# Conditioning blocks of a decoder layer: four visits of eight in place of six of five and six

## The chip, the cores and the metric

The kernel runs on one core of a Trainium2 chip. The metric is the device time of one execution in microseconds; the time before is the median of three runs. One more execution was profiled, and every row below comes from its trace.

## What is computed

One inference step of a one-layer decoder for 256 prompt tokens and 8 x 4 sample tokens (288 columns), model width 2048, all in float32. Cut to what matters here:

```python
mod = (silu(c) @ w_ada + b_ada).reshape(n, 6, 1, 2048)      # c: 9 conditioning vectors
sh_m, sc_m, gt_m, sh_f, sc_f, gt_f = [mod[:, i] for i in range(6)]
h = rms(x, g_mix) * (1 + sc_m) + sh_m
b_gate, c_gate, hc, u, v, ga, gb = split(h @ w_in)
ya = b_gate * conv(c_gate * hc)                              # short causal convolution
yb = gelu(u) * (w_causal @ rms(gelu(v), g_v) + b_sg)         # mixing within chunks
merged = sigmoid(ga) * (ya @ w_pa) + sigmoid(gb) * (yb @ w_pb)
x = x + gt_m * (merged @ w_out)
h2 = rms(x, g_ffn) * (1 + sc_f) + sh_f
gate, up = split(h2 @ w_ffn_in)
x = x + gt_f * ((silu(gate) * up) @ w_ffn_out)               # then a last rms
```

`mod` has 96 tiles of 128 features. Tiles 32 to 47 are gt_m, wanted first by the residual behind w_out, and tiles 48 to 63 are sh_f.

## The kernel before

Features lie on the 128 partitions, tokens along the free dimension. Weights are streamed from HBM once. A main block (`Blk`) is a piece of a weight matrix of up to 16 tiles of 128 x 128, 1 MB. It is loaded into a buffer of the pool `raw` (`RAW = 7` buffers of 8 KB per partition, L28), and then split into a high and a low half in four quarters of four tiles: ScalarE casts the high half (L480), VectorE subtracts to get the low half (L487). For each half there are four buffers of one quarter (`SPB = 4`, L478 and L481), so the next block's quarters take over the buffers that the present block's matmuls give back. Each tile then makes three matmuls of 288 columns (L239, L242, L244), 48 in a block, and a sink on VectorE (L802 for the blocks around the change) takes the finished sum from PSUM.

A conditioning block (`Ada`) is 1 MB of `w_ada` too and takes a `raw` buffer, but it isn't split: four float32 matmuls of 512 columns (L412, eight instructions in the trace) read the raw buffer as it is, into column groups 0 to 3 of one accumulator `ada`. Units a2 (tiles 32 to 47) and a3 (tiles 48 to 63) have 16 blocks each. They are done in *visits*: a run of conditioning blocks between two main blocks. Units a4 and a5 are done in a visit of six and a later one of ten, whose last four blocks are fetched by `fetch` (L392) into other buffers (the pool `kept`).

What sets the order: `steps2` lists the main blocks of this stage (first two half blocks wE and wF, then wD, pa, pb, wo), and `at` puts `plan[n]` behind the n-th of them. PE's order is the order of the steps, by hand. The loads (SyncE, one queue), ScalarE and VectorE are put in order by the framework's planner here, from when a buffer would be free and by place in the program. The loop at the end walks over `stream`, all blocks with a `raw` buffer; at its i-th block it emits the load of `order[i + AHEAD]` (`AHEAD = RAW`), then the split of the next main block if that one has a load, then the block's matmuls. `order` is `stream` with four main blocks moved ahead of earlier conditioning units.

Among the steps of the visits stand three others: `v_stats` (row statistics of v, after the 9th main block), `half_gt` (halves gt_m, after the 15th) and `v_samples` (transposes v of the sample tokens and stores it, after the 28th).

Of the kernel before, what the change touches and what calls it, by code (L numbers as in the profile page):

```python
# [88 lines left out]
def decoder_kernel(tc, d):  # L89
    nc = tc.nc  # L90
    from contextlib import ExitStack

    with ExitStack() as es:
        def pool(name, bufs=1, **kw):
            return es.enter_context(tc.tile_pool(name=name, bufs=bufs, **kw))

        pc = pool("const")
        pw = pool("wstream")
        pslot = pool("slots", MAIN)
        pkept = pool("kept", KEPT)  # L100
        ptmp = pool("tmp", 5)
        pps = pool("psum", 4, space=bass.MemoryType.PSUM)
        with tc.manual_schedule(engines={nc.tensor.engine}):
            _body(tc, nc, d, pc, pw, pslot, pkept, ptmp, pps)


def _body(tc, nc, d, pc, pw, pslot, pkept, ptmp, pps):
# [482 lines left out]
    def ada(name):  # L590
        u = units[name]
        return [Ada(u, b) for b in range(16 // u[2])]
# [58 lines left out]
    def pre_h1(k0, k1):  # L651
        def scaled(k):
            def f():
                made[k] = normed(k, S["rb1"])

            return f

        return Do(lambda: jobs.extend(scaled(k) for k in range(k0, k1)), None)
# [91 lines left out]
    def mk_h1(k0, k1):  # L750
        def f():
            gm_of(k0, k1)
            if S.get("paced") is not None:
                return make_h1(k0, k1)
            modulate(range(k0, k1), lambda k: normed(k, S["rb1"]), gm1, 0, h1)

        return Do(f)
# [381 lines left out]
    plan = {4: [Do(root, None)], 5: aC[:2], 6: aC[2:5] + [pre_h1(2, 5)], 7: aC[5:] + [mk_h1(2, 5)]}  # L1139
# [17 lines left out]
    steps2 += [Blk("pb", i, yb.__getitem__, sink_pb) for i in range(8)]  # L1157
    steps2 += [Blk("wo", i, mg.__getitem__, sink_wo) for i in range(16)]
    a2, a3, a4, a5 = ada("a2"), ada("a3"), ada("a4"), ada("a5")
    visits = [u[o:e] for u in (a2, a3) for o, e in ((0, 5), (5, 10), (10, 16))]  # L1160
    visits[1].insert(0, Do(v_stats, None))
    visits[2].append(Do(half_gt))
    visits[4].insert(0, Do(v_samples, None))
    plan = dict(zip((3, 9, 15, 21, 28, 35), visits))

    def apart(unit, plan, second, early):
        plan[second] = unit[6:]
# [19 lines left out]
    plan = {}  # L1187
# [12 lines left out]
    order = list(stream)  # L1200
    for unit, blk in ((aC[:2], wA[3]), (aC[2:5], wA[4]), (aC[5:], wA[5]), (aE[5:11], wC[0])):
        order.remove(blk)
        order.insert(order.index(unit[0]), blk)
    head = contextlib.ExitStack()
    head.enter_context(tc.manual_schedule(engines={A.engine, V.engine, SY.engine}))
    for s in stream[:2]:
# [21 lines left out]
    for s in steps:  # L1228
# [14 lines left out]
        i = pos[id(s)]  # L1243
# [124 lines left out]
```

## Time and profile before

| what | us |
|---|---|
| median of 3 runs | 1591.73 (1591.66 to 1592.06) |
| profiled execution | 1592.19 |
| its span, first to last instruction | 1590.40 |
| TensorE matmul (PE) busy | 1579.8 |
| VectorE (DVE) busy | 1014.4 |
| ScalarE (ACT) busy | 736.2 |

The mean granted clock of TensorE is 0.998 of full speed. In the rows below times are microseconds from the start of the span. A row of the timeline has its start, its length (for several alike instructions in a row the length of all), the engine, the line, the operation, what it writes and reads, the shapes and the count; in brackets stands the idle time of the engine ahead of it and what ended it. SPq is SyncE, which issues the loads. In the rows of a line of code "DMA to landing" is the time from the issue to the moment when the last byte is there, as minimum, median and maximum.

### The profile page before, as it was taken

What the parts mean: (1) busy time and instruction counts of PE and PEld (TensorE: products, weight loads), DVE (VectorE), ACT (ScalarE), POOL (GpSimd) and SP (SyncE); (2) the same over time, 40 slices, a digit from 0 to 9 for tenths busy, and PEclk for the clock granted to TensorE, in tenths of its full rate; (3) what the DMA queues carried; (4) which work ended last, traced back from release to release, by engine and by line L of the source; (5) the groups of instructions that cost most, each with busy time, mean ns of one, the idle gap of its engine ahead of it and who ended that gap; (6) DMA issues with size and microseconds to landing.
All of it is one profiled execution on the core that took longest, in us unless ns stands there. A gap on an engine that the chain in (4) does not pass through costs nothing.

```text
span 1590.4 us, 31810 instructions
## 1 busy us (share of the span) xinstructions
PE 1579.8 (99%) x12700; PEld 1519.9 (96%) x12700; DVE 1014.4 (64%) x2200; ACT 736.2 (46%) x1366; POOL 21.4 (1%) x65
## 2 busy tenths in 40 slices
PE   9999999999999999999999999999999999999997
PEld 8999899998999989899898999999999999999997
DVE  6777788877755758567844555555555555555565
ACT  6633344643444435356643444444444444444464
POOL 0000000000000000011000000000000000000000
PEclk9999999999999999999999999999999999999999
DMA  9887876777767778784757356453564534645341
GB/s 382 333 331 281 306 261 217 276 290 296 291 231 266 309 290 264 273 295 164 295 182 275 128 181 212 161 176 113 171 230 159 176 120 164 231 159 175 113 165 60
DMA packets 67685, 357.89 MB, mean 225 GB/s; under 512 B 7632, under 2 KB 19536, under 8 KB 37840
## 3 DMA queue, kind: packets, MB, share of 16 engines
q1 hardware_dynamic: 67248, 355.73, 61.6%
q8 instruction: 99, 1.62, 0.4%
q14 instruction: 50, 0.41, 0.1%
q10 hardware_dynamic: 288, 0.13, 0.0%
HBM read 352.74 MB, written 3.09 MB: 224 GB/s over the span
## 4 chain that ended last, share of the span: by engine, by line
PE 98%; DMA 1%; DVE 0%; DVEq 0%; ACT 0%; issue 0%; ACTq 0%
PE pm L239 31%; PE pm L244 31%; PE pm L242 30%; PE ada L412 5%; DMA raw<-in_wK 1%; DMA raw<-in_w 0%; DVE st L1079 0%; DMA t<-in_c 0%; PE px L242 0%; PE px L239 0%; PE px L244 0%; PE px L911 0%; PE px L910 0%; PE px L857 0%; PE px L213 0%; PE px L1051 0%
## 5 line engine op out<-in xcount | busy, mean ns | idle before, releaser
L239 PE MATMUL pm<-s,hi 128*128 128x288 f32 (+1 forms) x3750 | 1094.8, 292 | 0.0
L242 PE MATMUL pm<-s,hi 128*128 128x288 f32 (+1 forms) x3750 | 1090.5, 291 | 0.0
L244 PE MATMUL pm<-s,lo 128*128 128x288 f32 (+1 forms) x3738 | 1088.1, 291 | 0.0
L480 ACT CAST hi<-raw 128x512 fp32r<-128x512 f32 (+1 forms) x963 | 585.5, 610 | 777.9 <-PE pm L242 743.5
L487 DVE TENSOR_TENSOR lo<-raw,hi 128x512 fp32r<-128x512 f32 (+1 forms) x849 | 577.5, 682 | 408.6 <-ACT hi L480 396.1
L239 PEld LDWEIGHTS pm<-s,hi 128*128 128x128 f32 x3750 | 702.1, 187 | 11.7 <-issue 9.9
L242 PEld LDWEIGHTS pm<-s,hi 128*128 128x128 f32 x3750 | 702.2, 187 | 0.0
L244 PEld LDWEIGHTS pm<-s,lo 128*128 128x128 f32 x3738 | 699.9, 187 | 0.0
L258 DVE TENSOR_TENSOR lo<-raw,hi 128x512 fp32r<-128x512 f32 x111 | 74.4, 676 | 19.8 <-ACT hi L480 18.7
L412 PE MATMUL ada<-raw,cs 128*32 128x512 f32 (+2 forms) x1088 | 80.7, 444 | 1.0 <-DMA raw<-in_a 0.6
L412 PEld LDWEIGHTS ada<-raw,cs 128*32 128x32 f32 x1088 | 29.1, 110 | 41.9 <-issue 37.5
L802 DVE TENSOR_TENSOR s<-pm,s 128x288 f32<-128x288 f32 x72 | 32.8, 456 | 16.3 <-PE pm L244 16.1
L311 ACT CAST s<-t 128x288 fp32r<-128x288 f32 (+1 forms) x76 | 32.9, 433 | 15.6 <-DVE t L834 9.4
L313 DVE TENSOR_TENSOR s<-t,s 128x288 fp32r<-128x288 f32 (+1 forms) x76 | 35.0, 460 | 6.0 <-ACT s L311 5.2
L353 DVE SCALAR_TENSOR_TENSOR x<-pm,mod,x 128x256 f32<-128x256 f32 x79 | 37.6, 475 | 0.0
L1000 DVE SCALAR_TENSOR_TENSOR t<-t,pm 128x288 f32<-128x288 f32 x42 | 19.1, 455 | 19.6 <-PE pm L244 19.6
L794 DVE TENSOR_TENSOR s<-pm,s 128x288 f32<-128x288 f32 x48 | 21.8, 454 | 10.8 <-PE pm L244 10.0
L352 DVE TENSOR_TENSOR t<-pm,mod 128x32 f32<-128x32 f32 x79 | 15.1, 192 | 20.1 <-PE pm L244 19.5
L779 DVE SCALAR_TENSOR_TENSOR s<-pm,s 128x256 f32<-128x256 f32 x36 | 17.3, 481 | 8.3 <-PE pm L244 8.3
L785 DVE TENSOR_TENSOR s<-s,rb 128x288 f32<-128x288 f32 x48 | 21.6, 449 | 0.0
L181 ACT ACTIVATE t<-x 128x288 f32<-128x288 f32 x29 | 12.9, 444 | 17.6 <-DVE x L356 17.6
L186 DVE TENSOR_TENSOR acc<-acc,t 128x288 f32<-128x288 f32 x33 | 15.0, 455 | 8.2 <-ACT t L181 8.2
(170 smaller groups left out, 489.0 us busy)
## 6 DMA issues: line engine op xcount, KB each, us to landing
raw<-in_fi SPq DMA_DIRECT2D x84, 1024.0 KB, 4.8
raw<-in_a SPq DMA_DIRECT2D x56, 1024.0 KB, 5.0
raw<-in_f SPq DMA_DIRECT2D x64, 704.0 KB, 4.0
raw<-in_wD SPq DMA_DIRECT2D x34, 1024.0 KB, 6.7
raw<-in_aE SPq DMA_DIRECT2D x16, 1024.0 KB, 7.0
raw<-in_wo SPq DMA_DIRECT2D x16, 1024.0 KB, 6.0
raw<-in_wC SPq DMA_DIRECT2D x19, 768.0 KB, 6.5
raw<-in_pa SPq DMA_DIRECT2D x8, 1024.0 KB, 9.7
```

Source lines behind the costliest of these rows:

```text
L239: PE.matmul(out, wh, ah, start=first, stop=False)
L242: end_ = PE.matmul(out, wh, al, start=False, stop=turn and last)
L244: end_ = PE.matmul(out, wl, ah, start=False, stop=last)
L258: lows.pop(0)[1]()
L311: A.copy(hi, a)
L313: V.tensor_tensor(lo, a, hi.bitcast(F32), ALU.subtract)
L353: V.scalar_tensor_tensor(x[:, m, :TP], ps[:, :TP], mod[:, gt0 + m, 0:1], x[:, m, :TP], ALU.mult, ALU.add)
L412: PE.matmul(acc[32 * j : 32 * j + 32, h * w // n : (h + 1) * w // n], cs[:, kt, :], self.held[2 * j + h] if self.held else self.raw[:, o : ...
L480: A.copy(hi, self.raw[:, s * 128 : e * 128])
L487: sub()
L794: return V.tensor_tensor(part[m], ps[:, :T], part[m], ALU.add)
L802: V.tensor_tensor(a, ps[:, :T], a, ALU.add)
```

## The change

The 16 blocks of a2 and of a3 are done in two visits of eight each, behind main blocks 9 and 15 (a2) and 28 and 35 (a3). The visits behind main blocks 3 and 21 are gone. `v_stats`, `half_gt` and `v_samples` keep their places. In the load order, the main block behind each visit is moved ahead of the visit's first conditioning block.

```diff
     a2, a3, a4, a5 = ada("a2"), ada("a3"), ada("a4"), ada("a5")
-    visits = [u[o:e] for u in (a2, a3) for o, e in ((0, 5), (5, 10), (10, 16))]
-    visits[1].insert(0, Do(v_stats, None))
-    visits[2].append(Do(half_gt))
-    visits[4].insert(0, Do(v_samples, None))
-    plan = dict(zip((3, 9, 15, 21, 28, 35), visits))
+    visits = [u[o:e] for u in (a2, a3) for o, e in ((0, 8), (8, 16))]
+    visits[0].insert(0, Do(v_stats, None))
+    visits[1].append(Do(half_gt))
+    visits[2].insert(0, Do(v_samples, None))
+    plan = dict(zip((9, 15, 28, 35), visits))
...
         order.remove(blk)
         order.insert(order.index(unit[0]), blk)
+    for unit in (a2[:8], a2[8:], a3[:8], a3[8:]):
+        i = order.index(unit[-1]) + 1
+        order.insert(order.index(unit[0]), order.pop(i))
```

## Rows read from the trace of the kernel before

**Rows 1.** The page: busy times; the chain by engine; the casts (busy, mean ns)

```profile
PE 1579.8 (99%) x12700; PEld 1519.9 (96%) x12700; DVE 1014.4 (64%) x2200; ACT 736.2 (46%) x1366; POOL 21.4 (1%) x65
PE 98%; DMA 1%; DVE 0%; DVEq 0%; ACT 0%; issue 0%; ACTq 0%
L480 ACT CAST hi<-raw 128x512 fp32r<-128x512 f32 (+1 forms) x963 | 585.5, 610 | 777.9 <-PE pm L242 743.5
```

**Rows 2.** Waits of PE, whole span, largest on a load: total, times, longest (us)

```profile
PE ada L412 <- DMA raw<-in_a: 0.6, 1, 0.6
```

**Rows 3.** Timeline of PE around the visit of five blocks behind main block 21

```profile
413.30 0.29 PE L244 MATMUL pm<-s,lo 128*128 128x288 f32 x1
413.52 4.50 PE L412 MATMUL ada<-raw,cs 128*32 128x512 f32 x40
417.95 0.40 PE L239 MATMUL pm<-s,hi 128*128 128x288 f32 x1
418.19 0.29 PE L242 MATMUL pm<-s,hi 128*128 128x288 f32 x1
```

**Rows 4.** Timeline of PE around the visit of six blocks behind main block 15

```profile
370.71 5.36 PE L412 MATMUL ada<-raw,cs 128*32 128x512 f32 x48
376.00 0.40 PE L239 MATMUL pm<-s,hi 128*128 128x288 f32 x1
```

**Rows 5.** SP's waits, 440 to 466; then two loads, 452.5 and 458.7, to landing

```profile
SPq L463 <- DVE lo L487: 17.4, 3, 5.8
...
DMA to landing us min/median/max: 4.7/4.8/4.8
```

**Rows 6.** Timeline of DVE and PE at the start of two visits (413.52, 463.96)

```profile
415.10 0.69 DVE L487 TENSOR_TENSOR lo<-raw,hi 128x512 fp32r<-128x512 f32 x1
...
463.96 1.04 PE L412 MATMUL ada<-raw,cs 128*32 128x512 f32 x8
...
464.18 1.10 DVE L487 TENSOR_TENSOR lo<-raw,hi 128x512 fp32r<-128x512 f32 x1
465.20 0.47 DVE L884 SCALAR_TENSOR_TENSOR s<-px,r,s 128x256 f32<-128x256 f32 x1
```

**Rows 7.** First two loads inside three visits, timeline of PE and SP, line L463

```profile
328.74 1.07 PE L412 MATMUL ada<-raw,cs 128*32 128x512 f32 x8
329.87 0.33 SPq L463 DMA_DIRECT2D raw<-in_wD  x1
...
L463 SPq DMA_DIRECT2D raw<-in_wD x2: 328/356/383, 329.9 to 330.3; - x2
DMA to landing us min/median/max: 4.9/5.9/7.0
...
L463 SPq DMA_DIRECT2D raw<-in_wD x2: 328/328/328, 371.8 to 372.7; - x2
DMA to landing us min/median/max: 4.7/6.1/7.5
...
L463 SPq DMA_DIRECT2D raw<-in_wD x2: 327/354/382, 465.3 to 466.2; - x2
DMA to landing us min/median/max: 5.0/6.0/7.1
```

**Rows 8.** DVE in the visit behind block 3 and after it: stretch, length, busy

```profile
286.20:290.60 4.40, 3.35 (x10) 1.00 0.51 158
290.60:328.70 38.10, 33.69 (x74) 1.00 0.74 286
```

**Rows 9.** Timeline of PE in a4's visit of ten blocks

```profile
657.78 5.36 PE L412 MATMUL ada<-raw,cs 128*32 128x512 f32 x48
...
666.52 0.40 PE L239 MATMUL pm<-s,hi 128*128 128x288 f32 x1
```

**Rows 10.** PE at the end: stretch, length, busy, granted clock, DMA share, GB/s

```profile
1582.20:1585.00 2.80, 0.00 (x0) 1.00 0.72 277
1585.00:1586.00 1.00, 0.00 (x0) 0.60 1.02 407
```

## The prediction

> **What bounds the kernel now.** I read the busy times first, then the chain that ended last, then the waits of PE, then the timeline around the visits. TensorE is the kernel: it is busy 1579.8 of 1590.4 us and the chain lies on it for 98% [rows 1]. Over the whole span it waited for a load once, a conditioning matmul, 0.6 us [rows 2], at the start of the kernel; in the stretch that is changed it waits for nothing. So nothing can be gained there by making a wait shorter. Time can only come from work that PE no longer does, and any wait that the change makes for PE is added to the end in full, since no later slack exists to take it back.
>
> **What a visit costs PE.** A visit of five blocks starts at 413.52 and the next main matmul at 417.95 [rows 3], 4.43 us; a visit of six takes 370.71 to 376.00, 5.29 us [rows 4]. The difference, 0.86 us, is one block, and the rest of a visit is fixed: from the last main matmul before (413.30) to the second one after (418.19) pass 4.89 us [rows 3], of which five blocks are 4.30 and two ordinary matmul steps 0.26 (six main blocks lie between 376.00 and 413.52 [rows 3, 4], so a main block is 6.25 us and one of its 48 steps 0.13). That leaves **0.33 us per visit** for going into conditioning matmuls and out again. The change has two visits fewer and the same 32 blocks: -0.66 us. That is its whole gain on PE.
>
> **What the transfers cost.** A block of conditioning is 1 MB that PE uses up in 0.86 us. A lone 1 MB transfer takes 4.7 to 4.8 us from issue to landing [rows 5]. So a visit runs from what already lies in the seven raw buffers, and the question is how many of its eight blocks can lie there.
>
> Count them at the moment the visit starts. Between visits SP issues one load per main block, released by the last low half (L487) of a main block (three of them on L463 in those 26 us) [rows 5]: the raw buffer of a main block comes free only when its split is done, and its last quarter waits for a high/low buffer that the matmuls of the block before give back. In the visit at 463.96 this last quarter begins at 464.18, in the one at 413.52 at 415.10 [rows 6], after the visit's start in both. So when a visit starts, one of the seven buffers still holds the main block that follows. Before, the other six hold five or six conditioning blocks, and all are there. After, the main block is put ahead of the eight in the load order, so six blocks (1 to 6) are in and **blocks 7 and 8 have no buffer**. Their loads can be issued only when the visit itself frees one.
>
> When that is, the trace shows: the first load inside a visit leaves at 329.87, 371.8 and 465.3 for visits that start at 328.74, 370.71 and 463.96 [rows 4, 6, 7]. In the first two that is 1.13 and 1.1 us after the start, when the visit's first block, 0.86 us long, has drained; in the third it is 1.3 us, at the end of the low half [rows 6]. It lands 4.7 to 5.0 us later, and the second load lands 2.4 us (330.3 + 7.0 against 329.9 + 4.9), 3.7 us (372.7 + 7.5 against 371.8 + 4.7) and 3.0 us (466.2 + 7.1 against 465.3 + 5.0) after the first [rows 7]. I take 1.13 + 4.8 for block 7 and 3.0 more for block 8 (the middle of the three). Now against PE, from the visit's start:
>
> Block 7 is wanted at 6 x 0.86 = 5.16 and lands at 5.93: PE waits 0.8 us, then works 0.86. Block 8 lands at 8.93 where without waits PE would have started it at 7 x 0.86 = 6.02. **PE is 2.9 us late at the end of each visit**, and four visits make +11.6 us.
>
> The bounds of that: with the fast ends (4.7 and 2.4) block 8 lands at 8.2 and the visit loses 2.2 us; with the slow ones (first issue 1.34 as at 465.3, 5.0 and 3.7) it lands at 10.0 and loses 4.0 us. Four visits: +8.8 to +16.
>
> A sentence on what a page says: the Trainium skill, "DMA: Bandwidth & Descriptors", section "Rules for kernel authors", advises to issue a transfer early and wait for it late, so that its fixed part is hidden, and its section "Anatomy of one DMA" (for transfers issued by GpSimd) puts that part at about 2.0 us and the moving at 436 GB/s. That speaks against this change, which issues the last two loads of each visit when PE is already on it. By the page's figures a lone 1 MB would be an estimated 4.4 us, not the 4.8 of the rows, and the forecast would come out 1.6 us lower.
>
> **The other parts.** The move of the main block ahead of its unit costs PE nothing: its split needs it one main block earlier, and its load, one of the one-per-block loads of [rows 5], is in long before. What it costs is the buffer counted above. The main block after it is loaded behind block 8: it lands some 2.4 to 3.7 us after it, about 12 us into the visit, and PE wants its halves only after the block in between, 6.2 us after the visit's end at about 9.8, that is at 16; a cast (0.61) and a low half (0.69) take 1.3 us together [rows 1, 6], so this is hidden with over 2 us left. The v_stats, half_gt and v_samples steps stand at the same main blocks as before (9, 15 and 28), so PE and DVE do them where they did; v_samples' store stands among SP's loads at that visit and waits for DVE until 465.67 [rows 6], 1.7 us into it, which can push block 8's issue there (not block 7's, which left ahead of it, at 465.3): inside the bounds.
>
> The visit after block 3 also gave DVE a rest. In it DVE did 3.35 us of work that had piled up from the gelu tiles [rows 8]. Without it that work must go beside the main blocks up to the next visit, where DVE was busy 33.69 of 38.10 us [rows 8], so 4.4 us are free. It fits, tightly, and a late low half has 4.7 us of room (three quarters of a block, 1.56 us each, that are still split ahead of PE), so I take 0. If it comes too late, what piled up bounds the cost: 0 to +3.35 us. The visit after block 21 is followed by blocks that only add and take a tanh, and I take 0 there too.
>
> **The sum.** -0.66 + 11.6 = +10.9 us. Against the profiled execution, 1592.19 us (span 1590.40 and 1.79 around it), that is 1603.1; that execution lies 0.46 us above the median of the runs, 1591.73, so for the median **1602.7 us**, 0.7% slower.
>
> **The rivals.**
>
> *One buffer more than I count* (it ends on the other side). If the last quarter of the main block's split were done before the visit, block 7 would be in, and block 8 would leave at 1.13 and land at 5.93, before 6.02: no wait at all, and the two visits that are gone leave 1591.1 us. It decides at a landing of 6.02 us. For it: the margin is one buffer, and a ten-block visit passes without any wait, 657.78 to 666.52, ten blocks in 8.74 us [rows 9], when its blocks are there (`fetch`, L392, brings its last four to other buffers). Against it: the low half lies behind the visit's start in both visits shown [rows 6], and one quarter of a split needs a buffer that only the end of the main block frees. Chance 0.10.
>
> *DVE becomes late* in the blocks after the lost visit, on top of the forecast: up to +3.35, 1606.0 us. For it: 4.4 us free against 3.35 [rows 8]. Against it: the 4.7 us of room. Chance 0.08.
>
> *The clock falls.* With these gaps PE is idle for 0.8 us and soon after for 2.1 us. At the end of the kernel PE stands still from 1582.2, the granted clock is 1.00 up to 1585 and 0.60 in the next microsecond, that is on its way from 2.4 to 1.2 GHz [rows 10]; so 2.8 us of standing still did not lower it by itself. If it fell in each of the four visits, a main block at half clock costs 6.2 us more, at most 25 us in all: up to 1627 us. The Trainium skill has this as a rule ("TensorE: Matmul & The Clock Gate", section "HAM oscillation — how this bites in real kernels"): matmul bursts parted by waits for transfers can fall back to half rate at each wait. By that rule 1627; by the row, no fall. Chance 0.07.
>
> *The move doesn't take effect*: the planner leaves the main block behind its unit in SP's order. Then seven conditioning blocks are in, block 8 leaves at 1.13 and lands in time, but the main block lands about 3 us behind it, at 8.9, and its first halves are ready 1.3 us later, at 10.2, where PE wants them at 8 x 0.86 + 0.14 = 7.0. That is 3.2 us per visit and 1603.9 us, with another wait in the profile. Chance 0.05.
>
> **How the numbers follow.** The forecast has 0.70. Its own bounds are 1591.73 - 0.66 + 8.8 to 16, 1599.9 to 1607.1 us. The range should hold 8 in 10: 1597 to 1609 takes in the forecast, late DVE and the move without effect (0.83), with some room below for a visit that does not starve; outside lie the clock and the extra buffer. A measurement of this kernel can tell about 0.2% (3.2 us) from no change. Slower by more: 0.70 + 0.08 + 0.07 + 0.05 = 0.90, less 0.02 for the forecast coming out too small to be told, 0.88. The extra buffer (0.10) falls within, save 0.02 for a gain beside the visits that no row shows; with the 0.02 of the forecast that makes 0.10 within and 0.02 faster.
>
> **What would show it.** In the waits of PE there should be conditioning matmuls waiting for their own transfers, eight waits in four visits, 0.8 and 2.1 us each, about 11.6 us in sum; each visit should last about 9.9 us, not 7.0, with its load issues 1.1 us and about 2 us after its start. DVE's low halves should not release PE. If PE waits instead for low halves right behind the visits, the move had no effect; if after block 3, DVE is late; if there is no wait and the visits last 7.0 us, my count of the buffers is wrong; if main matmuls take 0.26 us a step behind the visits, it is the clock. The prediction falls if the time stays below 1597.

## The result and the profile after

The changed kernel takes 1604.93 us (median of six executions, 1601.94 to 1607.05), the kernel before beside it 1591.89: a ratio of 1.0079, 95% interval 1.0066 to 1.0092, that is 13.0 us slower. 1602.7 was forecast. The profiled execution took 1604.7 us, its span is 1602.9, 12.5 us longer than before.

The page first, as in [rows 1]: PE's busy time and the chain's shares.

```profile
PE 1582.7 (99%) x12700; PEld 1520.3 (95%) x12700; DVE 1010.8 (63%) x2200; ACT 736.0 (46%) x1366; POOL 21.9 (1%) x65
PE 95%; DMA 3%; DVE 1%; ACT 0%; issue 0%; POOL 0%; DVEq 0%; ACTq 0%; SPq 0%
```

The same 12700 matmuls, 2.9 us more of busy time (1579.8 before), and a chain that lies on transfers for 3% where it was 1% (the chain counts such a load whole, from its issue, with the time in which PE still worked). Where [rows 2] had one wait for a load, at the start, the waits of PE from 25 us on to the end now have one entry, eight times:

```profile
PE ada L412 <- DMA raw<-in_a: 10.1, 8, 2.6
```

The timeline of PE through three of the four visits shows where they are (behind main blocks 9, 15 and 35; start, length, and in brackets the idle time ahead of the row):

```profile
323.98 5.36 PE L412 MATMUL ada<-raw,cs 128*32 128x512 f32 x48
330.30 1.06 PE L412 MATMUL ada<-raw,cs 128*32 128x512 f32 x8 [0.96 <-DMA raw<-in_a]
332.73 1.58 PE L412 MATMUL ada<-raw,cs 128*32 128x512 f32 x8 [1.36 <-DMA raw<-in_a]
334.23 0.61 PE L239 MATMUL pm<-s,hi 128*128 128x288 f32 x1
334.64 0.44 PE L242 MATMUL pm<-s,hi 128*128 128x288 f32 x1
334.88 0.44 PE L244 MATMUL pm<-s,lo 128*128 128x288 f32 x1
...
372.82 5.36 PE L412 MATMUL ada<-raw,cs 128*32 128x512 f32 x48
378.82 1.07 PE L412 MATMUL ada<-raw,cs 128*32 128x512 f32 x8 [0.64 <-DMA raw<-in_a]
382.52 1.06 PE L412 MATMUL ada<-raw,cs 128*32 128x512 f32 x8 [2.64 <-DMA raw<-in_a]
383.52 0.40 PE L239 MATMUL pm<-s,hi 128*128 128x288 f32 x1
...
520.50 5.36 PE L412 MATMUL ada<-raw,cs 128*32 128x512 f32 x48
526.52 1.06 PE L412 MATMUL ada<-raw,cs 128*32 128x512 f32 x8 [0.66 <-DMA raw<-in_a]
528.93 1.06 PE L412 MATMUL ada<-raw,cs 128*32 128x512 f32 x8 [1.35 <-DMA raw<-in_a]
529.93 0.40 PE L239 MATMUL pm<-s,hi 128*128 128x288 f32 x1
```

In every visit 48 instructions, six blocks, run in one piece as in [rows 4], then block 7 waits and block 8 waits. From the visit's first matmul to the next main one pass 10.25, 10.70 and 9.43 us here, and 9.88 in the visit behind block 28 (466.86 to 476.74). Without waits it would be 7.00 (a run below shows this length), so the four visits are 12.3 us late. The 10.1 us of the row are less, because it counts a wait from the end of the matmul before. Blocks that follow each other without a gap overlap by 0.2 us (one is 1.06 us long, and one comes every 0.86 us); eight gaps lose this overlap too, 1.6 us, and the rest is the clock, below. The loads of blocks 7 and 8 in the visits at 323.98 and 372.82, the counterpart of [rows 7] (count, first and last issue; then issue to landing, minimum, median, maximum):

```profile
L385 SPq DMA_DIRECT2D raw<-in_a x2: 328/356/384, 325.1 to 325.5; - x2
DMA to landing us min/median/max: 5.1/6.1/7.2
...
L385 SPq DMA_DIRECT2D raw<-in_a x2: 327/328/328, 374.0 to 375.1; - x2
DMA to landing us min/median/max: 4.8/6.1/7.4
```

Block 7 leaves 1.1 to 1.2 us after the visit's start in both and is there at 6.2 and 6.0; block 8 lands 2.5 us (325.5 + 7.2 against 325.1 + 5.1) and 3.7 us (375.1 + 7.4 against 374.0 + 4.8) after it.

One thing more is in the first of these timelines. Its block 8 takes 1.50 us up to the next main matmul (332.73 to 334.23), that of the second visit 1.00 (382.52 to 383.52), and the main matmuls behind it step by 0.24 us, not 0.13. The stretches of PE (length, busy, granted clock, DMA share, GB/s), behind this visit and behind the second:

```profile
330.30:333.10 2.80, 1.44 (x12) 1.00 1.02 433
333.10:336.60 3.50, 3.50 (x18) 0.51 1.00 424
336.60:340.00 3.40, 3.40 (x28) 1.00 1.02 429
...
382.50:386.00 3.50, 3.48 (x27) 1.00 1.00 419
```

From 333.1 to 336.6 TensorE has half its clock, 1.2 of 2.4 GHz. Block 8 loses 0.5 us by it and the main matmuls up to 336.6 another 1.1 (2.3 us at 0.24 a step instead of 0.13). So 12.3 us late, of which 0.5 is the clock, 1.1 us of clock behind the visit, and -0.66 us for the two visits that are gone: 12.7, against 12.5 in the span.

### The profile page after: what moved, and what is told of

Same layout as the page of the kernel before. It is cut to its first block, busy times and chain, and to the rows that moved or that the text cites. A ratio compares the mean times of both kernels' runs of the same rounds, so it can differ in the third digit from the quotient of the medians.

```text
span 1602.9 us, 31819 instructions
## 1 busy us (share of the span) xinstructions
PE 1582.7 (99%) x12700; PEld 1520.3 (95%) x12700; DVE 1010.8 (63%) x2200; ACT 736.0 (46%) x1366; POOL 21.9 (1%) x65
## 4 chain that ended last, share of the span: by engine, by line
PE 95%; DMA 3%; DVE 1%; ACT 0%; issue 0%; POOL 0%; DVEq 0%; ACTq 0%; SPq 0%
PE pm L239 30%; PE pm L244 30%; PE pm L242 30%; PE ada L412 4%; DMA raw<-in_a 2%; DMA raw<-in_wA 1%; DMA raw<-in_w 0%; DMA cp<-in_cpack 0%; DVE st L1079 0%; DVE lo L487 0%; PE px L239 0%; PE px L242 0%; PE px L244 0%; PE px L911 0%; PE px L910 0%; ACT hi L480 0%
## 5 line engine op out<-in xcount | busy, mean ns | idle before, releaser
L802 DVE TENSOR_TENSOR s<-pm,s 128x288 f32<-128x288 f32 x72 | 32.6, 454 | 11.8 <-PE pm L244 11.6
L426 DVE STREAM_TRANSPOSE ev<-ada 128x512 f32<-128x512 f32 (+2 forms) x9 | 4.8, 536 | 34.8 <-PE ada L412 34.8
```

Source lines behind the costliest of these rows:

```text
L802: V.tensor_tensor(a, ps[:, :T], a, ALU.add)
```

## The experiments

Theory A is the prediction's: the loss is the wait for the two blocks that find no raw buffer, now with the clock as a second term. Theory B: the move of the main block costs. Theory C: the longer or lost visits cost something of their own. Ratios stand against runs of the kernel before on the same chip.

**Without the move.** The loop that moves the main block ahead of its unit is left out.

```diff
-    for unit in (a2[:8], a2[8:], a3[:8], a3[8:]):
-        i = order.index(unit[-1]) + 1
-        order.insert(order.index(unit[0]), order.pop(i))
```

> The changed kernel without the move of the main block in the load order; visits of eight stay. Theory A (seven raw buffers, whoever is eighth or ninth in the load order waits): seven conditioning blocks are in at the start of a visit, block 8 leaves about 1.1 us after it and lands at 5.9, in time for 6.0, so conditioning matmuls wait for nothing; but the main block behind the visit lands about 3 us later (8.9) and PE waits for its low half at 10.2 where it wanted it at 7.0. Four waits of about 3.2 us, +12 us, near 1604, and PE's waits name the low half, not the load of a conditioning block. Theory B (the move is what costs): without it the two lost visits remain, 1591.2 us.

1607.34 us, ratio 1.0096 (1.0081 to 1.0112). PE's waits over the whole span:

```profile
PE pm L239 <- ACT hi L480: 8.2, 4, 2.1
PE ada L412 <- DMA raw<-in_a: 1.5, 3, 0.6
...
PE pm L244 <- DVE lo L487: 0.6, 3, 0.2
```

The wait moved as expected, from the conditioning blocks to the main block behind each visit; the row names the cast, which the first main matmul needs ahead of the low half, so that part of the expectation was loose. Block 8 still waited in two of the visits, 0.5 us. The time is 3.4 us above what was expected, and the granted clock shows why: it is at half speed behind three of the four visits, not behind the one at 382.3 (the same columns as above):

```profile
334.10:337.60 3.50, 3.50 (x14) 0.51 0.99 419
...
382.30:386.00 3.70, 3.46 (x24) 1.00 1.01 425
477.50:481.00 3.50, 3.50 (x17) 0.51 1.01 426
532.10:535.60 3.50, 3.50 (x18) 0.51 1.02 433
```

Theory B falls: without the move the kernel is not faster. Eight blocks and the block behind them are nine loads for seven buffers, in either order.

**Blocks 7 and 8 without a load.** `twin` makes a block read the raw buffer of another one.

```diff
+            if self.twin:
+                self.raw = self.twin.raw
+                return
...
+    for u in (a2, a3):
+        for k in (6, 7, 14, 15):
+            u[k].twin = u[k - 6]
```

> The changed kernel, but blocks 7 and 8 of each visit load nothing and read the raw buffers of blocks 1 and 2 of the same visit, so part of the conditioning is computed from wrong weights; the same matmuls run. Theory A (all of the loss is the waiting for these two loads, with any fall of the clock that the waits bring): no waits in the visits, full clock, and the saving of two visits remains: -0.66 us, near 1591.2. Theory C (visits of eight, or the lost visits behind main blocks 3 and 21, cost something of their own, through VectorE or the clock): clearly above 1592, up to 1596.

1591.82 us, ratio 1.0000 (0.9992 to 1.0009). No wait of PE between 25 and 1580 us, and the visit runs through:

```profile
324.64 7.07 PE L417 MATMUL ada<-raw,cs 128*32 128x512 f32 x64
331.65 0.40 PE L239 MATMUL pm<-s,hi 128*128 128x288 f32 x1
```

7.01 us for eight blocks, 7.00 in the visit behind block 35, full clock throughout. Theory C falls: visits of eight, the two lost visits, the tighter VectorE and the move cost nothing that can be told. The 0.66 us of the lost visits don't show in the median; the interval is 1.4 us to each side. The traces show them. The last matmul of main block 3 and the first one behind the last visit, in the kernel before and then here:

```profile
286.00 0.29 PE L244 MATMUL pm<-s,lo 128*128 128x288 f32 x1
517.40 0.40 PE L239 MATMUL pm<-s,hi 128*128 128x288 f32 x1
...
286.53 0.29 PE L244 MATMUL pm<-s,lo 128*128 128x288 f32 x1
517.25 0.40 PE L239 MATMUL pm<-s,hi 128*128 128x288 f32 x1
```

Between the two pass 231.40 us before and 230.72 here, 0.68 less. What comes ahead of main block 3's end took 0.53 us longer in this execution, and that hides it. In the changed kernel the same stretch takes 244.06 us (285.87 to 529.93), 12.66 more than before, so the whole loss arises there.

**Only block 7 without a load.** The same with `for k in (6, 14)`: a case of one buffer more.

> As the kernel whose blocks 7 and 8 read other buffers, but only block 7 of each visit does so (its part of the conditioning is wrong); block 8 is loaded. It makes the case of one raw buffer more. Theory A: the load of block 8 is now the first inside the visit, leaves at 1.1 to 1.3 us, lands at 5.9 to 6.2 where PE wants it at 6.0: waits of 0 to 0.3 us, 1591.1 to 1592.2 us in all. If the loss were not set by the count of buffers but by loads being slow beside conditioning matmuls, block 8 would still come near 8.9 and the kernel would take about 1600.

1593.83 us, ratio 1.0013 (1.0004 to 1.0022): 1.6 us above the expected end. Three visits waited and one did not. The timeline of PE in the visits behind main blocks 15 and 35:

```profile
369.09 6.21 PE L417 MATMUL ada<-raw,cs 128*32 128x512 f32 x56
376.20 1.07 PE L417 MATMUL ada<-raw,cs 128*32 128x512 f32 x8 [0.90 <-DMA raw<-in_a]
...
511.98 7.13 PE L417 MATMUL ada<-raw,cs 128*32 128x512 f32 x64
519.04 0.40 PE L239 MATMUL pm<-s,hi 128*128 128x288 f32 x1
```

and block 8's load in each, issue and landing:

```profile
L390 SPq DMA_DIRECT2D raw<-in_a x1: 328/328/328, 371.4 to 371.4; - x1
DMA to landing us min/median/max: 4.8/4.8/4.8
...
L390 SPq DMA_DIRECT2D raw<-in_a x1: 328/328/328, 513.4 to 513.4; - x1
DMA to landing us min/median/max: 4.6/4.6/4.6
```

The expectation had overlooked that block 7, reading block 1's buffer, holds that buffer for six blocks more. So block 8's load waited for another buffer and left 2.3 us after the visit's start in the one visit (371.4 less 369.09) and 1.4 in the other (513.4 less 511.98). In the visit behind main block 9 it left in time, 0.9 us after the start (324.6 less 323.68), but took 6.0 us, and PE waited 0.67 us. The load that left at 513.4 landed at 518.0, 6.0 us after the start, and PE didn't wait: within the tenth to which these times are given, the point at which the prediction had said this case decides.

**Block 7 reading block 6's buffer.** As before, but `u[k].twin = u[k - 1]`, so block 1's buffer is free after block 1.

> As the kernel whose block 7 alone loads nothing, but block 7 reads the buffer of block 6, not of block 1 (part of the conditioning is wrong), so block 1's buffer is free at its end and not six blocks later. The run with block 1's buffer lost 0.7 to 1.1 us in three visits, since there the load of block 8 waited for a low half or for block 2. Theory A: the load now leaves at 1.1 us where the planner gives it block 1's buffer and lands at 5.8 to 6.2, where 6.02 is wanted: 0 to 0.2 us per visit, 1591.2 to 1592.0. If the planner still gives it the main block's buffer, waits of up to 1 us remain in that visit.

1591.88 us, ratio 1.0000 (0.9991 to 1.0009). The visits take 7.21, 7.00, 7.11 and 7.00 us; in the second, from 368.55 to 375.55, the load of block 8 left at 369.7, 1.1 us in:

```profile
L390 SPq DMA_DIRECT2D raw<-in_a x1: 328/328/328, 369.7 to 369.7; - x1
DMA to landing us min/median/max: 4.7/4.7/4.7
```

It landed at 374.4, 5.9 after the start. In the first visit it left at 324.9, took 5.0 us and landed 6.1 after the start (323.80), and that is the visit of 7.21 us. One load less, with block 1's buffer free in time, takes the loss away to within 0.2 us a visit, though block 8 is still loaded inside the visit: block 8 has 6.02 us for that.

**Visits of 6, 6 and 4, with the move.**

```diff
-    visits = [u[o:e] for u in (a2, a3) for o, e in ((0, 5), (5, 10), (10, 16))]
+    visits = [u[o:e] for u in (a2, a3) for o, e in ((0, 6), (6, 12), (12, 16))]
...
+    for u in (a2, a3):
+        for o, e in ((0, 6), (6, 12), (12, 16)):
+            i = order.index(u[e - 1]) + 1
+            order.insert(order.index(u[o]), order.pop(i))
```

> The kernel before with visits of 6, 6 and 4 for each unit (not 5, 5 and 6), at the same six places, and with the main block behind each visit moved ahead of it in the load order. Theory A: with the main block in one buffer, six conditioning blocks fill the other six, so nothing waits: 1591.9 us, as before, within 0.3. Theory B (the move costs by itself): some us above, with waits in visits of six.

1591.78 us, ratio 1.0000 (0.9991 to 1.0009), and PE waits for nothing between 25 and 1580 us. The move by itself costs nothing as long as six blocks follow it.

**Visits of 7, 7 and 2, with the move.** The same with `((0, 7), (7, 14), (14, 16))`.

> The kernel before with visits of 7, 7 and 2 for each unit at the same six places, the main block behind each visit moved ahead. Theory A: one block too many in each of four visits, wanted at 5.16 us and there at about 5.9 to 6.2: start-to-start 0.8 to 1.1 us late each, 3.2 to 4.4 us, near 1595.5 (fewer if the planner's first free buffer comes late), between 6, 6, 4 (no wait) and 8, 8 (2.9 us per visit). If waits grew with the number of blocks in a visit in any other way, or if the clock made the loss, seven would be near 1592 or near 1600.

1595.71 us, ratio 1.0025 (1.0015 to 1.0034): +3.9 us, in the middle of the 3.2 to 4.4 expected. From 25 to 1580 us PE waits four times, 3.4 us in all, each time a conditioning matmul for its load; two of them in the timeline:

```profile
292.05 1.06 PE L412 MATMUL ada<-raw,cs 128*32 128x512 f32 x8 [0.80 <-DMA raw<-in_a]
...
337.01 1.07 PE L412 MATMUL ada<-raw,cs 128*32 128x512 f32 x8 [0.52 <-DMA raw<-in_a]
```

So six cost nothing, seven about 1 us per visit, eight about 3: the steps that the count of buffers gives. The seventh block of a visit comes too late where, above, a lone eighth came in time, because it is wanted 0.86 us sooner. None of these gaps lowered the clock in the profiled execution.

**The change for a2 alone.** Two visits of eight behind main blocks 9 and 15, a3 in 5, 5 and 6.

```diff
+    visits = [a2[:8], a2[8:]] + [a3[o:e] for o, e in ((0, 5), (5, 10), (10, 16))]
...
+    plan = dict(zip((9, 15, 21, 28, 35), visits))
```

> The change for a2 alone (two visits of eight behind main blocks 9 and 15); a3 stays with 5, 5 and 6 behind 21, 28 and 35. Theory A: what the two visits lose in the profile of the changed kernel (6.3 us, start to start) less 0.33 for one visit gone, and the clock fall that this profile shows in the first of them, 0 to 1.9: 1597.8 to 1599.7 us, and no wait in a3's visits. If a loss in one visit were taken back or passed on by a later one, the two would not add up.

1599.39 us, ratio 1.0049 (1.0035 to 1.0062): +7.6 us, inside what was expected, with no wait in a3's visits. In this execution the clock fell behind the second visit, not the first; it shows in the timeline of PE as the time from block 8 to the next main matmul, 1.00 us in the first and 1.23 in the second:

```profile
332.38 1.07 PE L412 MATMUL ada<-raw,cs 128*32 128x512 f32 x8 [1.35 <-DMA raw<-in_a]
333.38 0.40 PE L239 MATMUL pm<-s,hi 128*128 128x288 f32 x1
...
381.08 1.31 PE L412 MATMUL ada<-raw,cs 128*32 128x512 f32 x8 [2.90 <-DMA raw<-in_a]
382.31 0.61 PE L239 MATMUL pm<-s,hi 128*128 128x288 f32 x1
```

Losses add up visit by visit, and which visit loses its clock is not fixed by the place.

**Work for TensorE in the waits.** Small bf16 matmuls into a spare PSUM tile, 5 ahead of block 7 and 9 ahead of block 8.

```diff
+            if self.ahead:
+                warm(self.ahead, psmisc())
...
+    for u in (a2, a3):
+        for k, f in ((6, 5), (7, 9), (14, 5), (15, 9)):
+            u[k].ahead = f
```

> The changed kernel with bf16 matmuls into a spare PSUM tile put on PE ahead of block 7 (5 of them) and block 8 (9) of each visit, so that TensorE has work for part of each wait; nothing else differs. At about 0.12 us each they fill 0.6 and 1.1 us, less than the waits of the trace (0.6 to 1.0 and 1.4 to 2.6 us). Theory A with the clock as a second term (the waits are the same in every execution, and what spreads the times from 1601.9 to 1607.1 us is the granted clock, which falls in none, one or two of the four visits, 1.7 to 1.9 us each): no stretch at the low clock in the visits, a spread under 1 us, and a median at the low end, 1601.9 to 1602.4. If the spread comes from the landing of the loads, it stays at some 5 us and the median near 1604.9.

1604.58 us (1603.06 to 1606.46), ratio 1.0081 (1.0067 to 1.0095). A miss: neither the median nor the spread came down as expected. The visit behind main block 9 kept its clock, the one behind 15 stood idle for 2.68 us in spite of the filling, and lost it (stretch, length, busy, granted clock):

```profile
334.00:337.40 3.40, 3.40 (x30) 1.00 1.01 427
382.60:386.00 3.40, 3.40 (x15) 0.50 1.00 424
```

Block 8's load in the visit behind main block 15, issued at 373.8, took 8.6 us to land, against 7.4 in the changed kernel.

**The same with 27 in that place.** `a2[15].ahead = 27`.

> As the kernel with bf16 matmuls ahead of blocks 7 and 8 of each visit, but with 27 of them (not 9) ahead of block 8 in the visit behind main block 15, the one that still stood idle for 2.7 us there and then ran 3.4 us at the low clock. 27 x 0.13 is 3.5 us, against a wait of 3.9 us in that place. Theory A with the clock as second term: no stretch at the low clock in any visit, median 1602 to 1603, spread under 1.5 us. If the times still spread by 3 us or more at full clock, the spread comes from the landing of the loads.

1605.32 us (1604.52 to 1605.93), ratio 1.0083 (1.0069 to 1.0097). Half met. No visit runs at the low clock, and the five executions lie within 1.4 us, where the changed kernel's six spread over 5.1. But the median is 2 to 3 us above the expected one. The timeline of PE in that visit:

```profile
378.46 3.48 PE L606 MATMUL px<-wb 128*128 128x288 bf16 x27
381.87 1.06 PE L414 MATMUL ada<-raw,cs 128*32 128x512 f32 x8
```

Block 8's load, issued at 373.7, landed 7.3 us later, at 381.0; the 27 matmuls held PE until 381.87, so 0.9 us of the excess is the filling itself. In the visit behind block 28 block 8 started 9.76 us after the visit's start (8.89 in the changed kernel), and behind block 35 at 8.99 (8.43): in this execution the loads came later, and with full clock throughout. (Behind block 28 they also left later, block 7's 1.5 us after the visit's start and not 0.9.) Whether the filling itself delays the loads is not shown.

So the spread of the changed kernel has two parts, the clock and the landing of the loads. The mean granted clock of each execution is on record, to a thousandth, and 3.4 us at half clock take about 0.001 off a mean over 1603 us. The six executions are 1601.94 (0.998), 1602.41 (0.999), 1604.70 (0.997, the profiled one, with one fall), 1605.17 (0.997), 1606.37 (0.997) and 1607.05 (0.996); without the move all four have 0.995, and the profiled one of them has three falls. From this an estimate: the slowest and the fastest differ by about two falls, some 3.2 of the 5.1 us, and the 1.7 us between the three at 0.997 are left for the landings. Three digits tell no more: the profiled execution with the change for a2 alone has one fall and 0.998. Only one execution of each kernel has a trace.

## Why the prediction was right, point by point

- **What a visit costs and saves**: right, as far as it can be told. A visit of eight without waits took the 7.00 us that 8 x 0.86 + 0.14 gave. The saving of 0.66 us never showed in a median; between the same two matmuls of the traces it is 0.68 us.
- **The count of buffers** (six in, blocks 7 and 8 without one): right, and shown: six follow the moved block for nothing, seven and eight pay, and one load less takes it all away. That six fit had also been in the code: the units a4 and a5 take their first six blocks from raw buffers and fetch the last four of the ten-block visit elsewhere [rows 9].
- **The size of the waits**: 11.6 us forecast, 11.8 in the trace (12.3 less 0.5 of clock). Counted from start to start, as the prediction did, block 7 came 0.84 to 1.16 us late (0.8 forecast) and block 8 another 1.55 to 2.84 (2.1). The 3.7 us between two landings, taken as the slow end from the visit behind main block 15 [rows 7], came back in that same visit.
- **The point of decision of the rival with one buffer more**, 6.02 us: borne out to within a tenth by block 8 landing at 6.0 with no wait and at 6.1 with 0.2 us lost. The kernel that comes nearest to that case took 1591.88 us, against the 1591.1 given for it.
- **VectorE without its rest**: right with 0. Its low halves release no wait of PE between main blocks 3 and 9.
- **The move without effect**: it had its effect, and the price given for the other case (1603.9) was right in its kind and 3.4 us short; the trace has three falls of the clock, which that price left out.
- **The clock**: the term that was mis-sized. It was put at 0 with a chance of 0.07, because PE had stood still for 2.8 us at the end of the kernel at full clock [rows 10]. In the profiled execution it fell behind one visit of four and cost 1.6 us; in the run without the move it fell behind three. The price of a fall in the prediction, a whole main block at half speed, was too high: here 2.3 us of main matmuls and half of a conditioning block ran at 1.2 GHz. The profiled execution lies 1.6 us above the 1603.1 worked out for it, as much as this one fall; the median lies 2.2 us above the forecast, and the two executions whose mean clock shows no loss against the kernel before, 1601.94 and 1602.41, lie beside it. The Trainium skill ("TensorE: Matmul & The Clock Gate", section "HAM oscillation — how this bites in real kernels") tells of waits for transfers that each lower the clock, but of longer waits than those here, so the 1627 that the prediction took from it goes further than it says. The trace agrees in kind: waits for transfers between bursts did lower the clock, though not at each wait.

No kernel here beats the one before. With eight blocks a visit only two come level with it, the one in which blocks 7 and 8 load nothing and the one in which block 7 reads block 6's buffer; with all loads done, visits of at most six do.

## What to carry to other kernels

Count the buffers at the moment a burst starts: those that still hold the next main block are not there for the burst, and where the burst uses a 1 MB block in 0.86 us, a new one took 4.6 us or more in every visit shown here. Moving another load ahead of the burst only changes which load is last; a load too many costs what its landing is late, in full, where the engine that waits is the whole chain. Price such a wait with what it does to the clock behind it, which one still stretch at the end of a kernel can't rule out.

## What was not expected of the hardware

- In one trace the clock fell after two gaps of 0.96 and 1.36 us with one block of conditioning between them, and not after gaps of 0.64 and 2.64 us 50 us later; in another (a2 alone) it was the other way round, after 0.84 and 2.90 us and not after 0.95 and 1.35; with work in the waits it fell after a single gap of 2.68 us. The length of a gap alone doesn't tell.
- Two 1 MB loads issued 0.4 us apart landed 2.4 to 2.5 us apart. Issued 1.1 us apart, in the visit behind main block 15, they landed 3.7 us apart. The transfers didn't slow down: in those 3.7 us they ran at 416 GB/s and moved 1.5 MB, where in the 2.5 us behind main block 9 they ran at 426 GB/s and moved 1.07. So nearly half a megabyte of the loads that were issued behind block 8's came in ahead of its last byte. Why there and not in the other visits was not tried.
